# A mixture-of-experts kernel on one core: the rows of x for experts 0 to 3 come in as f32 on SyncE's queue, with the casts on ScalarE

## Chip, core and metric

The kernel runs on one core of one Trainium2 chip. The metric is the time of one execution on the device in microseconds (us); less is better. Time before: 184.42 us, the median of 5 runs that lie between 183.97 and 184.64.

## The reference

Eight experts, each with its own two weight matrices and its own 256 rows of x; two matrix products with a ReLU between them. Everything is f32 on the outside.

```python
n_experts, capacity, hidden, expert_hidden = 8, 256, 512, 2048
# x [8, 256, 512], w1 [8, 512, 2048], w2 [8, 2048, 512]
h = np.matmul(x, w1)
h = np.maximum(h, 0)
return np.matmul(h, w2).astype(np.float32)
```

An expert's w1 and w2 hold 4 MB each, its rows of x 0.5 MB and its output 0.5 MB.

## The kernel before

**Computation.** All products are made in bf16 with f32 sums in PSUM. The experts go one after the other. `first_layer(e)` (matmuls at L105) makes the hidden rows of expert e, transposed, in 64 matmuls, with ReLU on the way out of PSUM by ScalarE and VectorE in turn (L115, L113). `second_layer(e)` (L125) makes the output in 32 matmuls into two PSUM tiles, which VectorE and ScalarE copy to an f32 tile (L136, L137). The experts 5, 6 and 7 do their first layers together ahead of their second layers.

**Weights.** Each w1 and w2 is loaded by the gpsimd queue with the cast from f32 to bf16 made in the transfer (L70, L76), into pools of three buffers each (`WB = 3`). w2 of experts 6 and 7 is cut in 2 and 6 pieces. Because all of these are issued by GpSimd, they stand in one ring, in the order of the program; so do the outputs of experts 0 to 6 (`store`, L140). This ring is called the gpsimd ring below. The output of expert 7 is stored in two halves by SyncE and ScalarE.

**x.** The rows of x are handled in four groups, `GROUPS = ((0, 1), (1, 1), (2, 2), (4, 4))`: expert 0, expert 1, experts 2 and 3, experts 4 to 7. Group 0 is loaded as f32 by SyncE into `x_f` (L143) and cast to bf16 by one ScalarE copy (L154). Groups 1, 2 and 3 are loaded by the gpsimd ring with the cast in the transfer (`load_x`, L66), in rows of 4, 8 and 16 KB of f32 per partition, among the weights. `transpose_x(g)` then turns a group with TensorE (L86) through PSUM, with copies out by VectorE and ScalarE (L95, L93).

**Order.** The schedule is manual: each engine executes its instructions in the order in which the program calls them. What GpSimd is told to load first is first in the ring:

```python
    nc.sync.dma_start(x_f[:], x_rows(0))
    load_w1(0)
    make_identity(nc, identity)
    load_x(1)
    load_w2(0)
    load_w1(1)
    load_x(2)
    load_w2(1)
    load_x(3)
    load_w1(2)
    load_w2(2)
    nc.scalar.copy(x_b[0][:], x_f[:])
    transpose_x(0)
```

Later loads are issued when the buffer that they fill is free: `load_w1(3)` after `first_layer(0)`, `load_w2(3)` after `second_layer(0)`, and so on. Output tiles come from the pool `outs` of four buffers; five are used in all, for the experts (0, 1), (2, 3), (4, 5), (6) and (7).

Of the kernel before, what the change touches and what calls it, by code (L numbers as in the profile page):

```python
# [10 lines left out]
def kernel(  # L11
# [7 lines left out]
    nc = tc.nc  # L19
    P = 128  # L20
    bf = mybir.dt.bfloat16
    f32 = mybir.dt.float32
    relu = mybir.ActivationFunctionType.Relu

    E, C, H = x.shape
    F = w1.shape[2]
    MT = C // P
# [14 lines left out]
    const = ctx.enter_context(tc.tile_pool(name="const", bufs=1))  # L42
    wpool = ctx.enter_context(tc.tile_pool(name="weights", bufs=WB))
    hpool = ctx.enter_context(tc.tile_pool(name="hidden", bufs=3))
    opool = ctx.enter_context(tc.tile_pool(name="outs", bufs=4))
    ps_h = ctx.enter_context(tc.tile_pool(name="ps_h", bufs=4, space=bass.MemoryType.PSUM))
    ps_o = ctx.enter_context(tc.tile_pool(name="ps_o", bufs=4, space=bass.MemoryType.PSUM))

# [2 lines left out]

    w1_sb, w2_sb, ht, o_sb = {}, {}, {}, {}
    group_of = {e: g for g, (e0, n) in enumerate(GROUPS) for e in range(e0, e0 + n)}
    x_f = const.tile([P, MT, H], f32, name="x_f")
    x_b = [const.tile([P, n * MT, H], bf, name=f"x_b{g}") for g, (_, n) in enumerate(GROUPS)]
    xt = [const.tile([P, KT1, n, C], bf, name=f"xt{g}") for g, (_, n) in enumerate(GROUPS)]
    identity = const.tile([P, P], bf, name="identity")
# [1 line left out]
    def x_rows(g):  # L59
        e0, n = GROUPS[g]  # L60
        return x[e0:e0 + n].rearrange("e c k -> (e c) k").rearrange(
            "(p j) k -> p j k", p=P
        )

    def load_x(g):
        nc.gpsimd.dma_start(x_b[g][:], x_rows(g))  # L66

    def load_w1(e):
        w1_sb[e] = wpool.tile([P, KT1, F], bf, tag="w1", name="w1_sb")
        nc.gpsimd.dma_start(w1_sb[e][:], w1_r[e])  # L70

    def load_w2(e):
        w2_sb[e] = wpool.tile([P, KT2, H], bf, tag="w2", name="w2_sb")
        cuts = {E - 2: (0, 8, 16), E - 1: (0, 5, 9, 12, 14, 15, 16)}.get(e, (0, KT2))
        for lo, hi in zip(cuts, cuts[1:]):
            nc.gpsimd.dma_start(w2_sb[e][:, lo:hi, :], w2_r[e, :, lo:hi, :])  # L76

    def transpose_x(g, kts=range(KT1)):


        n = GROUPS[g][1]
        J = n * MT
        for kt in kts:
            pt = ps_o.tile([P, J, P], bf, tag="ps_o", name="pt_tr")
            for j in range(J):
                nc.tensor.transpose(pt[:, j, :], x_b[g][:, j, kt::KT1], identity[:])  # L86
            src = pt[:].rearrange("p (j m) (e l) -> p m e l j", m=MT, e=n)
            for mt in range(MT):
                dst = xt[g][:, kt, :, mt * P:(mt + 1) * P].rearrange(
                    "p e (l j) -> p e l j", j=J // MT  # L90
                )
                if mt % 2:
                    nc.scalar.copy(dst, src[:, mt])  # L93
                else:
                    nc.vector.tensor_copy(dst, src[:, mt])  # L95
# [44 lines left out]
        nc.gpsimd.dma_start(out_r[:, es[0]:es[-1] + 1], o_sb[es][:, :len(es)])  # L140


    nc.sync.dma_start(x_f[:], x_rows(0))  # L143
    load_w1(0)
    make_identity(nc, identity)
    load_x(1)
    load_w2(0)
    load_w1(1)
    load_x(2)
    load_w2(1)  # L150
    load_x(3)
    load_w1(2)
    load_w2(2)
    nc.scalar.copy(x_b[0][:], x_f[:])  # L154
    transpose_x(0)

    first_layer(0)
# [66 lines left out]
```

## Time and profile before

| | |
|---|---|
| median of 5 runs | 184.42 us |
| the profiled execution | 184.42 us, of which the span from the first to the last instruction is 182.6 us |
| DMA | 40.22 MB written, HBM read 71.30 MB; gpsimd ring (q0) 97.4% of 16 engines' span |
| PE (matmul) busy | 127.1 us, 70% of the span |
| VectorE, ScalarE, GpSimd busy | 32.9, 31.2 and 16.8 us |
| mean granted TensorE clock | 0.939 |

The DMA queues of a core share 16 DMA engines. In the profile q0 is the gpsimd ring, q1 SyncE's queue, q10 ScalarE's, q8 and q14 the fetches of instructions and tables. A DMA is split in packets, one per partition's row here, and each of the 16 engines carries 8 of 128 partitions; the transfer has landed when the slowest engine has finished its share. GB/s and packet sizes count what is written: a transfer that casts to bf16 reads twice what it writes.

### The profile page before, as it was taken

The page shows a single profiled execution, that of the slowest core. Times are in us where ns is not written, and L with a number is a line of the kernel's source. Part 1 is how long each engine was busy: PE and PEld are TensorE (multiplying, and loading weights), DVE is VectorE, ACT ScalarE, POOL GpSimd, SP SyncE. Part 2 cuts the span into 40 slices and gives each one's busy share as a digit, 9 for nine tenths or more (in the row PEclk, how much of TensorE's full clock was granted, in tenths as well). Part 3 has the DMA queues.
Part 4 walks back from the last instruction along what each step waited for, and adds up shares of the span by engine and source line. Part 5 has one row for each costly group of instructions (what it writes and reads, how often), then busy time and mean ns, then how long its engine had stood idle before and what let it go on. Part 6 is the DMA issues. An engine that isn't in the chain of part 4 may idle for free.

```text
span 182.6 us, 1887 instructions
## 1 busy us (share of the span) xinstructions
PE 127.1 (70%) x832; PEld 89.1 (49%) x832; DVE 32.9 (18%) x56; ACT 31.2 (17%) x58; POOL 16.8 (9%) x35
## 2 busy tenths in 40 slices
PE   0205979499492099996859493965989494997980
PEld 0104864189240079636824491424979493443430
DVE  0100340113301015402400041010334132010110
ACT  3300240113201014303300230011222131010110
POOL 7301010100102000100000006011010100110100
PEclk9999999969998559999999998798799999999998
DMA  6999999999999999999999999999999999999993
GB/s 165 212 196 223 222 223 219 190 233 219 203 228 215 219 222 215 205 219 222 223 205 219 219 189 321 229 223 208 208 223 230 208 206 313 225 210 212 214 337 138
DMA packets 5001, 40.22 MB, mean 220 GB/s; under 512 B 513, under 2 KB 769, under 8 KB 2817
## 3 DMA queue, kind: packets, MB, share of 16 engines
q0 software_dynamic: 4560, 39.06, 97.4%
q1 hardware_dynamic: 288, 0.79, 1.2%
q10 hardware_dynamic: 144, 0.26, 0.4%
q8 instruction: 6, 0.10, 0.2%
q14 instruction: 3, 0.02, 0.0%
HBM read 71.30 MB, written 4.19 MB: 413 GB/s over the span
## 4 chain that ended last, share of the span: by engine, by line
DMA 51%; PE 33%; another core or an unknown queue 9%; POOL 2%; issue 1%; ACT 0%; POOLq 0%
DMA w_sb<-in_w_dram 51%; PE pt_o L125 19%; PE pt_h L105 13%; PE pt_tr L86 1%; POOL w_sb L76 1%; POOL w_sb L70 1%; POOL x_b L66 1%; POOL out_dram L140 0%; ACT out_sb L137 0%; POOL identity masks.py:199 0%; POOL identity masks.py:197 0%; POOLq L208 0%
## 5 line engine op out<-in xcount | busy, mean ns | idle before, releaser
L105 PE MATMUL pt_h<-xt,w_sb 128*128 128x256 bf16 x512 | 65.4, 293 | 32.0 <-DMA w_sb<-in_w_dram 32.0
L105 PEld LDWEIGHTS <-w_sb 128*128 128x128 bf16 x512 | 59.6, 147 | 38.2 <-DMA w_sb<-in_w_dram 35.2
L125 PE MATMUL pt_o<-w_sb,ht_sb 128*128 128x512 bf16 x256 | 57.9, 385 | 13.2 <-DMA w_sb<-in_w_dram 13.2
L125 PEld LDWEIGHTS <-ht_sb 128*128 128x128 bf16 x256 | 25.1, 99 | 44.3 <-issue 12.9
L113 DVE TENSOR_SCALAR ht_sb<-pt_h 128x512 bf16<-128x512 f32 x32 | 22.1, 692 | 75.9 <-PE pt_h L105 75.9
L115 ACT ACTIVATE ht_sb<-pt_h 128x512 bf16<-128x512 f32 x32 | 19.1, 598 | 68.3 <-PE pt_h L105 68.3
L136 DVE COPY out_sb<-pt_o 128x512 f32<-128x512 f32 x8 | 5.5, 692 | 63.5 <-PE pt_o L125 63.5
L137 ACT COPY out_sb<-pt_o 128x512 f32<-128x512 f32 x8 | 4.7, 585 | 66.4 <-PE pt_o L125 66.4
L76 POOL DMA_DIRECT2D w_sb<-in_w_dram x14 | 7.5, 536 | 69.3 <-DMA w_sb<-in_w_dram 41.5
L70 POOL DMA_DIRECT2D w_sb<-in_w_dram x8 | 4.5, 560 | 72.4 <-PE pt_h L105 51.8
L86 PE MATMUL pt_tr<-identity,x_b 128*128 128x128 bf16 x64 | 5.4, 238 | 5.1 <-ACT x_b L154 5.1
L86 PEld LDWEIGHTS <-x_b 128*128 128x128 bf16 x64 | 4.9, 120 | 5.2 <-ACT x_b L154 5.1
L93 ACT COPY xt<-pt_tr 128x128 bf16<-128x128 bf16 (+2 forms) x16 | 5.4, 376 | 9.3 <-DVE xt L95 9.3
L95 DVE COPY xt<-pt_tr 128x128 bf16<-128x128 bf16 (+2 forms) x16 | 5.6, 384 | 5.6 <-PE pt_tr L86 5.6
L140 POOL DMA_DIRECT2D out_dram<-out_sb x4 | 2.7, 678 | 13.2 <-ACT out_sb L137 12.9
L66 POOL DMA_DIRECT2D x_b<-in_x_dram x3 | 1.7, 563 | 0.0
L154 ACT ACT_TABLE_LOAD x1 | 1.3, 1283 | 0.7 <-PEq L208 0.7
L154 ACT CAST x_b<-x_f 128x1024 bf16<-128x1024 f32 x1 | 1.0, 1044 | 2.0 <-DMA x_f<-in_x_dram 2.0
masks.py:199 POOL TENSOR_SCALAR_AFFINE_SELECT identity<-identity 128x128 bf16<-128x128 bf16 x1 | 0.3, 287 | 0.1
masks.py:197 POOL MEMSET identity<- 128x128 bf16 x1 | 0.2, 223 | 0.0
L208 POOL MEMSET const-float32-0.0<- 128x1 f32 x1 | 0.1, 93 | 0.2 <-issue 0.2
L208 POOL MEMSET const-bfloat16-1.0<- 128x1 bf16 x1 | 0.1, 95 | 0.0
(2 smaller groups left out, 0.2 us busy)
## 6 DMA issues: line engine op xcount, KB each, us to landing
w_sb<-in_w_dram POOLq DMA_DIRECT2D x14, 2048.0 KB, 47.3
out_dram<-out_sb POOLq DMA_DIRECT2D x3, 1024.0 KB, 45.6
w_sb<-in_w_dram POOLq DMA_DIRECT2D x2, 1024.0 KB, 51.4
x_b<-in_x_dram POOLq DMA_DIRECT2D x1, 1024.0 KB, 48.4
w_sb<-in_w_dram POOLq DMA_DIRECT2D x1, 640.0 KB, 47.8
x_f<-in_x_dram SPq DMA_DIRECT2D x1, 512.0 KB, 3.3
x_b<-in_x_dram POOLq DMA_DIRECT2D x1, 512.0 KB, 34.9
w_sb<-in_w_dram POOLq DMA_DIRECT2D x1, 512.0 KB, 46.5
```

The lines of the kernel that those rows point to most:

```text
L66: nc.gpsimd.dma_start(x_b[g][:], x_rows(g))
L70: nc.gpsimd.dma_start(w1_sb[e][:], w1_r[e])
L76: nc.gpsimd.dma_start(w2_sb[e][:, lo:hi, :], w2_r[e, :, lo:hi, :])
L86: nc.tensor.transpose(pt[:, j, :], x_b[g][:, j, kt::KT1], identity[:])
L93: nc.scalar.copy(dst, src[:, mt])
L95: nc.vector.tensor_copy(dst, src[:, mt])
L105: nc.tensor.matmul(ph[:, i, :], w1_sb[e][:, kt, 2 * q + i::KT2], xe[:, kt, :], start=(kt == 0), stop=(kt == KT1 - 1),)
L113: nc.vector.tensor_relu(ht[e][:, 2 * q:2 * q + 2, :], ph[:])
L115: nc.scalar.activation(ht[e][:, 2 * q:2 * q + 2, :], ph[:], relu)
L125: nc.tensor.matmul(po[mt][:], ht[e][:, kt, mt * P:(mt + 1) * P], w2_sb[e][:, kt, :], start=(kt == 0), stop=(kt == KT2 - 1),)
L136: nc.vector.tensor_copy(o[:, 0, :], po[0][:])
L137: nc.scalar.copy(o[:, 1, :], po[1][:])
```

## The change

- SyncE loads two transfers instead of one: experts 0 and 1 (1 MB, two rows of 4 KB per partition), then experts 2 and 3 (1 MB, one row of 8 KB per partition), both f32 into a tile `x_f` four times as large as before.
- ScalarE makes four casts instead of one, in a row, ahead of the transposes of group 0: expert 0, expert 1, and experts 2 and 3 in two halves. All have 1024 elements per partition.
- `load_x(1)` and `load_x(2)` leave the gpsimd ring. `load_x(3)`, for experts 4 to 7, stays.
- The pool of output tiles has three buffers instead of four.

```diff
-    opool = ctx.enter_context(tc.tile_pool(name="outs", bufs=4))
+    opool = ctx.enter_context(tc.tile_pool(name="outs", bufs=3))
...
-    x_f = const.tile([P, MT, H], f32, name="x_f")
+    x_f = const.tile([P, 4, MT, H], f32, name="x_f")
...
-    nc.sync.dma_start(x_f[:], x_rows(0))
+    nc.sync.dma_start(x_f[:, :2], x[0:2].rearrange("e (p mt) k -> p e mt k", p=P))
+    nc.sync.dma_start(x_f[:, 2:].rearrange("p e mt k -> p (e mt) k"), x_rows(2))
     load_w1(0)
     make_identity(nc, identity)
-    load_x(1)
     load_w2(0)
     load_w1(1)
-    load_x(2)
     load_w2(1)
     load_x(3)
     load_w1(2)
     load_w2(2)
-    nc.scalar.copy(x_b[0][:], x_f[:])
+    nc.scalar.copy(x_b[0][:], x_f[:, 0])
+    nc.scalar.copy(x_b[1][:], x_f[:, 1])
+    for j in (0, 1):
+        nc.scalar.copy(x_b[2][:, 2 * j:2 * j + 2, :], x_f[:, 2 + j])
     transpose_x(0)
```

## The prediction

> **What bounds the kernel now.** I read the page first (busy slices, DMA queues), then the chain of waits in order of time, then the timeline of the first microseconds, then windows over the start, then the single DMA records (packets and per-engine landings). All clock times are us from the start of the span.
>
> The page, slices and queues:
>
> ```profile
> PE   0205979499492099996859493965989494997980
> DMA  6999999999999999999999999999999999999993
> q0 software_dynamic: 4560, 39.06, 97.4%
> q1 hardware_dynamic: 288, 0.79, 1.2%
> ```
>
> The DMA engines are full in every slice but the first and the last; PE has holes all along. 97.4% of the engines' time is the gpsimd ring.
>
> The end of the chain of waits (start, us, what):
>
> ```profile
> 112.20 49.65 DMA w_sb<-in_w_dram
> 161.85 0.04 issue
> 161.90 3.61 PE pt_o L125 x16
> 165.51 1.21 another core or an unknown queue
> 166.72 0.04 issue
> 166.76 10.60 PE pt_o L125 x48
> ```
>
> Each late layer starts when its weights land, 0.04 to 0.05 us after the landing (166.72 to 166.76). The last 48 matmuls run without a gap, but from a landing; so if every landing of w1(7), w2(5) and w2(6) moves by some amount, the end moves by it. The landings are those of the slowest of 16 engines. From the landing records: w2(6)'s second half has landed on the fastest engine at 163.34, on the median at 164.52, on the slowest at 166.72. That lag of 3.4 us is built up thus: 2.15 us are there when w1(0) lands (13.73 fastest, 13.95 median, 15.71 and 15.88 the two slowest); it stays between 2.13 and 2.15 up to x of experts 4 to 7 (51.36 to 53.50); it grows by 0.96 while w1(2) lands; and by about 0.3 later, around 103 to 113.
>
> The timeline of the start, the lines that matter, with SP's DMA, the cast and the first matmuls:
>
> ```profile
> 0.74 0.37 SPq L143 DMA_DIRECT2D x_f<-in_x_dram  x1
> 1.26 0.67 POOL L70 DMA_DIRECT2D w_sb<-in_w_dram  x1 [0.81 <-POOLq L208]
> 4.03 1.04 ACT L154 CAST x_b<-x_f 128x1024 bf16<-128x1024 f32 x1 [2.01 <-DMA x_f<-in_x_dram]
> 5.82 0.91 ACT L93 COPY xt<-pt_tr 128x128 bf16<-128x128 bf16 x4 [0.75 <-DVE xt L95]
> 15.92 9.37 PE L105 MATMUL pt_h<-xt,w_sb 128*128 128x256 bf16 x64 [9.76 <-DMA w_sb<-in_w_dram]
> ```
>
> PE waits 9.76 us for w1(0), with x long ready. And windows over the start (the last two columns are the DMA share and GB/s written):
>
> ```profile
> 1.70:3.20 1.50, 0.00 (x0) 0.00 (x0) 0.00 (x0) 0.32 (x1) 1.43 (x5) 1.00 1.10 347
> 3.20:4.70 1.50, 0.00 (x0) 0.00 (x0) 0.00 (x0) 0.67 (x1) 1.50 (x4) 1.00 1.05 199
> 4.70:8.00 3.30, 1.04 (x8) 0.78 (x8) 0.86 (x4) 1.28 (x5) 1.50 (x3) 1.00 1.01 199
> 8.00:16.00 8.00, 0.08 (x1) 0.08 (x2) 0.00 (x0) 0.00 (x0) 0.00 (x0) 1.00 1.02 213
> ```
>
> From 3.2 to 8 the ring moves 199 GB/s against 213 later. The packet records say why: x_f's packets end between 3.12 and 3.63 on the engines, w1(0)'s first packets start by 3.98 on fourteen of them and at 4.67 on the last two, which so stand still for over 1.0 us; and the early w1 packets take 1.25 to 2.45 us where later ones take 1.23.
>
> **The change part by part.**
>
> *The work of the engines.* Removed from the ring: x of expert 1 and of experts 2 and 3. Their price is the step between landings of the slowest engine: 15.88 to 17.12 = 1.24 us and 36.49 to 38.95 = 2.46 us, together 3.70 us. Added on SyncE's queue: per engine 8 more rows of 4 KB and 8 rows of 8 KB. x_f's packets start 0.155 us apart, so 8 of them are 1.24 us. An 8 KB row as f32 isn't in the trace on this queue; the nearest row is a table fetch of 8 KB (0.309 to 0.322 us), which gives 8 x 0.309 = 2.47. From below, 8 x 0.307 by the step of the casting rows. Sum 3.71: net 0.0 us. The cast saves no time, since the engines are paid by what they read (4096 B in 0.155 us, 8192 in 0.307, 32768 in 1.21: 26.4 to 27 B/ns).
>
> *Where it stands in time.* x's 3.7 us come ahead of or among w1(0), w2(0) and w1(1) instead of behind w1(0) and w1(1). So w1(0), landing at 15.88, comes up to 3.7 us later, w2(0) (26.81) and w1(1) (36.49) up to 2.5 later, and from w2(1) (48.64) on all is level. PE: first layer 0 takes 9.4, second 7.1, first layer 1 about 7.5 with its transposes; the next landing that must be met is w2(1) at 48.64 and then w1(2) at 64.16, for which PE now waits 8.4 us (55.76 to 64.16). The delay is gone there at the latest. Nobody feels it before: the loads w1(3) and w2(3) that wait for these layers are issued at 25.59 and 34.23, but reach the engines only after w1(2) and w2(2), from about 73.85 on. Price nothing; if the cover were gone, at most the 3.7.
>
> *The casts.* Three more of 1.04 us each on ScalarE, 3.1 us, in the 9 us in which it idles before w1(0). But the last two wait for the second transfer, and behind them in ScalarE's queue stand its copies for the transposes of group 0, which first_layer(0) needs, and its ReLUs. How late does that transfer land? If SyncE's packets go first, at about 1.75 + 16 x 0.155 + 8 x 0.309, some 7 to 8 us: hidden. If engines take a packet of each queue in turn (as the records show for SyncE's and ScalarE's stores at 179.6 to 180.9: 0.080 us each, strictly alternating on the late engines), some 15 rows still open at 3.2 to 3.6 go one by one with 1.21 us packets of w1(0) and w2(0): 3.4 + 15 x 1.21 + 3.7 = 25. Then first_layer(0) starts at about 25 + 2.1 + 1.6 = 29, and the chain 9.4 + 0.6 + 7.1 + 7.5 + 1.1 + 7.1 ends at about 62, still ahead of 64.16. Free in both cases, the second by 2 us; past that PE has some 2.5 us of waiting in each later layer (93.26, 102.90) to catch up.
> The Trainium skill ("DMA: Bandwidth & Descriptors", section "Queues, rings and completion order") says that each engine goes round its queues packet by packet, which would make it the second case.
>
> *The idle start.* The two slowest engines stand still for 1.0 to 1.2 us between the end of x_f and the first packet of w1(0). After the change they have 16 more rows of x (3.7 us) to move in that time. Gain: 0 if the stall holds all queues of the engine; 1.2 if it is filled; at the end no more than 1.5, since the third slowest engine is 1.5 us ahead there (175.23 against 176.71 for the last piece of w2). I take 1.2: idle time with queued work to fill it.
>
> *The mixing of queues.* About 15 rows of x are written between packets of the ring. Nearest rows: a table fetch of 8 KB at 149.76 between two ring packets delays the second by 0.354 us where it should cost 0.313, so 0.04 per row; at the other end an instruction fetch of 16 KB at 54.29 took 0.975 us and the ring's packet behind it 1.40 instead of 1.23, so 0.17 to 0.19 per row. 15 x 0.04 = 0.6; 15 x 0.19 = 2.9; a gain from mixing is the idle start, counted above. I take 0.6, since the 8 KB fetch has the size of a row.
>
> *Without price:* output tiles from three buffers: the tile of expert 6 reuses that of (0, 1), stored by 115.83, that of 7 the one of (2, 3), stored by 157.06; they are written at 170.2 and 177.2. SyncE's one more issue (0.37) and GpSimd's two fewer (0.55 each) lie at the start; fewer loads are queued in front of the ring, none of them late.
>
> Sum: 0.0 - 1.2 + 0.6 = -0.6 us; the profiled execution is 184.42, equal to the median: 183.8.
> The Trainium skill ("DMA: Bandwidth & Descriptors", section "Issuing engines are not separate DMA queues") speaks against any gain: transfers of all queues run on the same engines, and another issuer saves only issue time; by that alone the sum is 0.0 and the time 184.4.
>
> **The rivals.**
> *Nothing to be filled (0.24).* Net work 0.0 and the idle start and the mixing cancel or neither is real. For: the price per byte read is equal. Time 184.1 to 184.7.
> *Mixing costs more than the idle start gives (0.33).* Every row between two ring packets takes the reading ahead away from the ring, as behind the instruction fetch: 0.06 to 0.19 each on 15 rows, 0.9 to 2.9 us, with the stall filled only in part. It decides from 0.1 us per row on. Time 184.8 to 187, the middle about 185.5. For: packets after a foreign one measured 1.38 to 1.44 in four fetches. Against: SyncE's and ScalarE's stores alternate without loss.
>
> **How the numbers follow.** Forecast 183.8 with 0.43: gains from 0.4 to 1.5 us (182.9 to 184.0). Nothing 0.24, slower 0.33. 0.2% is 0.37 us, about what a measurement of this kernel can tell from no change. The range takes in the whole gain and the mixing up to half of its upper end: 182.9 to 185.9; the forecast's own is 182.9 to 184.0.
>
> **What would show it.** Right: w1(0) lands at 18 to 20; w2(1) lands up to 1 us before 48.6, the spread between fastest and slowest engine is near 1 us instead of 2.15, w2(6) lands 0.4 to 1.5 earlier, and the last 48 matmuls follow it. Wrong: a ring packet length of 1.3 to 1.4 while x runs, w2(1) after 48.9, and all later landings late by the same amount; or the two slow engines as late as before.

## The result, and the profile after

The changed kernel takes 183.25 us (median of 45 runs, 182.82 to 183.75) against 184.37 us for the kernel before (87 runs, 182.74 to 186.19). The ratio is 0.9944, with a 95% interval from 0.9934 to 0.9954: faster by 1.1 us. The forecast was 183.8 with a range from 182.9 to 185.9. One thing stands out beside the median: nine tenths of the runs before lie between 183.28 and 185.08, after between 182.95 and 183.54. The change made the kernel quicker, and its times scatter over a third of the width.

The profiled execution took 183.26 us, with a span of 181.1. First the page after, the DMA slices and the queues:

```profile
DMA  5998998999899999999999998999999999999994
q0 software_dynamic: 4272, 38.27, 95.6%
q1 hardware_dynamic: 560, 2.36, 3.6%
HBM read 71.30 MB, written 4.19 MB: 417 GB/s over the span
```

The two loading queues take 99.2% of the engines' time together, 98.6% before; what is read from memory is the same 71.30 MB, moved at 417 GB/s over the span instead of 413. Nothing was saved in bytes. The end of the chain of waits (start, us, what):

```profile
110.41 49.99 DMA w_sb<-in_w_dram
160.41 0.04 issue
160.45 3.61 PE pt_o L125 x16
164.06 1.15 another core or an unknown queue
165.22 0.04 issue
165.26 10.61 PE pt_o L125 x48
```

From 160.41 on it has the same pieces as before with nearly the same lengths, each 1.4 to 1.5 us earlier: w2(6) has landed at 165.22 instead of 166.72, and the last 48 matmuls start at 165.26 instead of 166.76. So the gain was made before these landings, in the transfers. The span became 1.5 us shorter, the time less: the part of an execution that lies outside the span (its time less its span) is 2.12 to 2.25 us in the runs of the changed kernel, and 1.74 to 1.85 in the runs of the kernel before beside the experiments. No run shows what makes this difference of 0.37 us.

The start shows what the transfers do, first in the timeline:

```profile
0.74 0.41 SPq L143 DMA_DIRECT2D x_f<-in_x_dram  x1
1.21 0.46 SPq L144 DMA_DIRECT2D x_f<-in_x_dram  x1
5.74 1.04 ACT L153 CAST x_b<-x_f 128x1024 bf16<-128x1024 f32 x1 [3.72 <-DMA x_f<-in_x_dram]
17.61 1.99 ACT L156 CAST x_b<-x_f 128x1024 bf16<-128x1024 f32 x2 [9.87 <-DMA x_f<-in_x_dram]
19.50 0.76 ACT L93 COPY xt<-pt_tr 128x128 bf16<-128x128 bf16 x4
19.81 9.00 PE L105 MATMUL pt_h<-xt,w_sb 128*128 128x256 bf16 x64 [11.93 <-ACT xt L93]
30.02 7.07 PE L125 MATMUL pt_o<-w_sb,ht_sb 128*128 128x512 bf16 x32 [0.76 <-ACT xt L93]
38.12 6.98 PEld L105 LDWEIGHTS <-w_sb 128*128 128x128 bf16 x64 [1.53 <-DMA w_sb<-in_w_dram]
```

The first layer begins 3.9 us later than before (19.81 instead of 15.92), and not because of w1(0): ScalarE waits 9.87 us for the second transfer of x, its transposition copies stand behind those casts, and PE waits for them. It costs nothing: by first_layer(1) PE's weight loads (PEld) wait for w1(1) again (1.53 us at 38.12). And the windows over the start (last two columns: DMA share, GB/s written; f32 rows count twice what a cast counts for the same bytes read):

```profile
3.20:4.70 1.50, 0.00 (x0) 0.00 (x0) 0.00 (x0) 0.00 (x0) 1.50 (x4) 1.00 1.02 418
4.70:8.00 3.30, 1.04 (x8) 0.78 (x8) 0.72 (x4) 1.99 (x2) 0.97 (x2) 1.00 1.13 317
8.00:16.00 8.00, 0.00 (x0) 0.00 (x0) 0.15 (x1) 0.00 (x0) 0.00 (x0) 1.00 0.98 249
```

In 3.20 to 4.70 the engines write f32 rows at 418 GB/s, where before the starting ring wrote 199 and so read 398.

The packet and landing records name the difference. All 4 KB rows of x go first, and on fifteen engines two of the 8 KB rows with them; the ring's first packets start between 5.36 and 5.90 us. Not one of them is long: before, 9 ring packets took over 1.5 us at the start (four of them over 2 us), after, none. The other 8 KB rows alternate one by one with them, an 8 KB row and a 16 KB ring packet together every 1.526 us, against 1.208 for the ring packet alone. w1(0) lands on the fastest engine at 17.51, on the slowest at 17.84: a spread of 0.33 us instead of 2.15. From w2(1) on the two kernels have moved the same bytes; there the median engine is level (46.72 against 46.80 before), the mean over the engines 0.33 earlier (46.77 against 47.10), and the slowest, which sets the landing, 0.87 earlier (47.77 against 48.64). At w2(6) the mean is 0.4 earlier (164.06 against 164.45) and the slowest 1.5.

### The profile page after: what moved, and what is told of

Read it like the earlier page. It is cut to its first block, busy times and chain, and to the rows that moved or that the text cites. A ratio compares the mean times of both kernels' runs of the same rounds, so it can differ in the third digit from the quotient of the medians.

```text
span 181.1 us, 1891 instructions
## 1 busy us (share of the span) xinstructions
PE 130.2 (72%) x832; PEld 90.4 (50%) x832; DVE 32.9 (18%) x56; ACT 34.0 (19%) x61; POOL 15.7 (9%) x33
## 3 DMA queue, kind: packets, MB, share of 16 engines
HBM read 71.30 MB, written 4.19 MB: 417 GB/s over the span
## 4 chain that ended last, share of the span: by engine, by line
DMA 47%; PE 39%; another core or an unknown queue 7%; POOL 2%; issue 1%; ACT 1%; DVE 1%; POOLq 0%
DMA w_sb<-in_w_dram 47%; PE pt_o L125 20%; PE pt_h L105 17%; PE pt_tr L86 1%; ACT xt L93 1%; POOL w_sb L76 1%; DVE ht_sb L113 0%; POOL out_dram L140 0%; ACT out_sb L137 0%; POOL w_sb L70 0%; DVE xt L95 0%; POOL identity masks.py:199 0%; POOL identity masks.py:197 0%; POOLq L210 0%
## 5 line engine op out<-in xcount | busy, mean ns | idle before, releaser
L105 PE MATMUL pt_h<-xt,w_sb 128*128 128x256 bf16 x512 | 66.3, 296 | 28.0 <-DMA w_sb<-in_w_dram 16.1
L105 PEld LDWEIGHTS <-w_sb 128*128 128x128 bf16 x512 | 60.3, 148 | 34.7 <-DMA w_sb<-in_w_dram 29.1
L125 PE MATMUL pt_o<-w_sb,ht_sb 128*128 128x512 bf16 x256 | 60.0, 395 | 10.8 <-DMA w_sb<-in_w_dram 8.4
L125 PEld LDWEIGHTS <-ht_sb 128*128 128x128 bf16 x256 | 25.7, 101 | 43.4 <-issue 15.1
L156 ACT CAST x_b<-x_f 128x1024 bf16<-128x1024 f32 x2 | 2.0, 1042 | 9.9 <-DMA x_f<-in_x_dram 9.9
L153 ACT CAST x_b<-x_f 128x1024 bf16<-128x1024 f32 x1 | 1.0, 1045 | 3.7 <-DMA x_f<-in_x_dram 3.7
L154 ACT CAST x_b<-x_f 128x1024 bf16<-128x1024 f32 x1 | 1.0, 1042 | 0.0
L66 POOL DMA_DIRECT2D x_b<-in_x_dram x1 | 0.6, 558 | 0.0
```

The costliest lines, as they stand in the source:

```text
L105: nc.tensor.matmul(ph[:, i, :], w1_sb[e][:, kt, 2 * q + i::KT2], xe[:, kt, :], start=(kt == 0), stop=(kt == KT1 - 1),)
L125: nc.tensor.matmul(po[mt][:], ht[e][:, kt, mt * P:(mt + 1) * P], w2_sb[e][:, kt, :], start=(kt == 0), stop=(kt == KT2 - 1),)
```

## The experiments

**The theories.** The *spread* of a load is the time between its landings on the fastest and the slowest engine; a *long* packet is a ring packet of over 1.5 us near the start. *Cover*: the gpsimd ring has a bad start, a few microseconds in which some engines begin late and packets take too long; rows of x on SyncE's queue give the engines work until that is over, and any rows would do. *Alternation*: the 8 KB rows between ring packets keep the engines even. *GpSimd*: the ring starts badly because GpSimd is issuing the next loads (2.46 to 6.2 us) meanwhile. *Leaving the ring*: what helps is that x is no longer in it.

**Each half alone.**

```diff
 e1_x01, against the kernel before:
-    x_f = const.tile([P, MT, H], f32, name="x_f")
+    x_f = const.tile([P, 2, MT, H], f32, name="x_f")
...
-    nc.sync.dma_start(x_f[:], x_rows(0))
+    nc.sync.dma_start(x_f[:, :2], x[0:2].rearrange("e (p mt) k -> p e mt k", p=P))
...
-    load_x(1)
...
-    nc.scalar.copy(x_b[0][:], x_f[:])
+    nc.scalar.copy(x_b[0][:], x_f[:, 0])
+    nc.scalar.copy(x_b[1][:], x_f[:, 1])
 e2_x23, against the kernel before:
-    opool = ctx.enter_context(tc.tile_pool(name="outs", bufs=4))
+    opool = ctx.enter_context(tc.tile_pool(name="outs", bufs=3))
...
-    x_f = const.tile([P, MT, H], f32, name="x_f")
+    x_f = const.tile([P, 3, MT, H], f32, name="x_f")
...
-    nc.sync.dma_start(x_f[:], x_rows(0))
+    nc.sync.dma_start(x_f[:, 0], x_rows(0))
+    nc.sync.dma_start(x_f[:, 1:].rearrange("p e mt k -> p (e mt) k"), x_rows(2))
...
-    load_x(2)
...
-    nc.scalar.copy(x_b[0][:], x_f[:])
+    nc.scalar.copy(x_b[0][:], x_f[:, 0])
+    for j in (0, 1):
+        nc.scalar.copy(x_b[2][:, 2 * j:2 * j + 2, :], x_f[:, 1 + j])
```

> Only half of the change: x of experts 0 and 1 as f32 on SyncE in one transfer (16 rows of 4 KB per engine), x of experts 2 and 3 cast on the gpsimd ring as before. Cover theory (the ring's start-up stall on single engines passes unseen while rows of SyncE's queue are on the engines): the gain is all here; w1(0) lands on all engines within 0.5 us (2.15 before), time 183.2 to 183.5. Theory of the alternation (the 8 KB rows written one by one between the ring's packets keep the engines even): these rows are gone, so the stall is back, spread of w1(0) 1.5 to 2.2 us, time 184.2 to 184.6. GpSimd theory (the stall comes from GpSimd writing the next loads' descriptors at 2.5 to 6.2 us while the ring starts): cured as far as the ring's first packet starts after 5 us; as it does, 183.2 to 183.5.

> The other half: x of expert 0 as before, x of experts 2 and 3 as f32 on SyncE in 8 KB rows, x of expert 1 cast on the gpsimd ring as before; output pool of 3 as in the changed kernel. Cover theory and alternation theory: cured, 183.2 to 183.5, spread of w1(0) under 0.5 us. GpSimd theory: the ring's first packets start at 3.4 to 4.6 us, in the middle of GpSimd's issues, so part of the stall stays: spread 1 to 2 us, time 183.8 to 184.5.

Measured: e1_x01 183.36 us, ratio 0.9961 (0.9943 to 0.9978); e2_x23 183.43 us, ratio 0.9958 (0.9939 to 0.9977); the kernel before on that chip 184.18. Each half does what the whole does within their intervals. The spread of w1(0) is 0.39 and 0.47 us, and neither has a long packet. The timelines show how differently they get there (e1_x01, then e2_x23: casts and first matmuls):

```profile
5.68 1.04 ACT L153 CAST x_b<-x_f 128x1024 bf16<-128x1024 f32 x1 [3.66 <-DMA x_f<-in_x_dram]
15.34 8.84 PE L105 MATMUL pt_h<-xt,w_sb 128*128 128x256 bf16 x57 [7.51 <-DMA w_sb<-in_w_dram]
```

```profile
10.46 1.99 ACT L156 CAST x_b<-x_f 128x1024 bf16<-128x1024 f32 x2 [5.26 <-DMA x_f<-in_x_dram]
16.48 7.69 PE L105 MATMUL pt_h<-xt,w_sb 128*128 128x256 bf16 x55 [10.19 <-DMA w_sb<-in_w_dram]
```

e1_x01 has no 8 KB rows and nothing that alternates, its x is through on each engine before the ring's first packet there (4.90 to 5.32 us), and its first layer starts even earlier than before (15.34): the alternation theory falls. In e2_x23 the ring's first packets start at 5.34 us with rows of x ahead of them. e1_x01 keeps four output buffers and e2_x23 has three, so the pool makes no visible difference.

**GpSimd's issues out of the way.**

```diff
 e4_gpwait, against the kernel before:
+    idle = const.tile([P, 2048], f32, name="idle")
...
     load_w1(0)
     make_identity(nc, identity)
+    for _ in range(3):
+        nc.gpsimd.memset(idle[:], 0.0)
     load_x(1)
```

> The kernel before, with GpSimd busy for some 5 to 6 us (three memsets of a scratch tile) between the identity and load_x(1): after load_w1(0) nothing more is issued on the ring until 8 us or so. GpSimd theory: w1(0)'s packets take 1.23 us from the first on, spread under 0.5 us, time 183.2 to 183.5. Cover theory: nothing covers the ring's start, spread 1.5 to 2.5 us as before, time 184.2 to 184.6; a plain loss would be possible only if the ring ran dry, which it does not before 13.7 us.

Measured: 184.84 us, ratio 1.0026 (1.0000 to 1.0053). In the kernel before, GpSimd issues six more loads from 2.46 us on, one after the other; the first and the last of them:

```profile
2.46 0.55 POOL L66 DMA_DIRECT2D x_b<-in_x_dram  x1
5.61 0.59 POOL L70 DMA_DIRECT2D w_sb<-in_w_dram  x1
```

The timeline of e4_gpwait shows the pause:

```profile
1.25 0.67 POOL L71 DMA_DIRECT2D w_sb<-in_w_dram  x1 [0.81 <-POOLq L211]
2.46 5.53 POOL L148 MEMSET idle<- 128x2048 f32 x3
8.49 0.54 POOL L77 DMA_DIRECT2D w_sb<-in_w_dram  x1
```

GpSimd issues no DMA from 1.9 to 7.9 us, and still two engines are late: w1(0) lands at 13.80 on the median engine, and on the last two at 15.27 and 16.59, the slowest 2.8 us behind the median (1.9, 2.5 and 0.4 in three profiles of the kernel before); the two longest early ring packets took 2.2 and 2.6 us. So the stall doesn't need GpSimd's issues. But there are only 3 long packets here, against 9 to 17 in the three profiles of the kernel before, so a part of the lengthening on the others may go with the issues; one profile doesn't show it.

**Rows that nobody needs.**

```diff
 e3_dummy, against the kernel before:
+    x_d = const.tile([P, MT, H], f32, name="x_d")
...
     nc.sync.dma_start(x_f[:], x_rows(0))
+    nc.sync.dma_start(x_d[:], x_rows(1))
```

> The kernel before with nothing moved, and 8 more rows of 4 KB per engine on SyncE's queue behind x_f: x of expert 1 is loaded a second time, into a tile that nobody reads; 1.24 us more work for every engine. Cover theory: the rows hide the ring's start, w1(0) lands on all engines within 0.5 us, and the time is 184.3 + 1.24 - 1.1 = 184.4 (184.1 to 184.7). Rival, that the gain comes from x leaving the ring (fewer or larger transfers in it): no gain, only the work, 185.5 (185.2 to 185.8), spread 1.5 to 2.5 us.

Measured: 184.37 us, ratio 1.0009 (0.9986 to 1.0032) to the kernel before (184.07). The windows of e3_dummy over the start:

```profile
3.20:4.70 1.50, 0.00 (x0) 0.00 (x0) 0.00 (x0) 0.77 (x1) 1.50 (x4) 1.00 1.66 505
4.70:8.00 3.30, 1.04 (x8) 0.78 (x8) 0.86 (x4) 1.18 (x5) 1.50 (x3) 1.00 0.81 169
8.00:16.00 8.00, 0.88 (x5) 0.71 (x6) 0.00 (x0) 0.00 (x0) 0.53 (x1) 1.00 1.09 227
```

Half a megabyte more to read, 1.24 us of every engine, and no measurable loss: it pays for itself. (A packet's whole time counts in the window where it starts, hence 1.66 and 0.81.) The rows last to 4.84 us, the ring's first packets follow at 4.47 to 4.84, no packet is long, and w1(0) lands with a spread of 0.48. Nothing has left the ring in this kernel, so that theory falls. With e1_x01 and e2_x23 this shows the gain to come with rows on SyncE's queue ahead of the ring's first packets; which rows they are doesn't matter.

**Is it the ring's first use, or the first microseconds of a run?**

```diff
 e7_latering, against the changed kernel:
+    idle = const.tile([P, 2048], f32, name="idle")
...
+    for _ in range(2):
+        nc.gpsimd.memset(idle[:], 0.0)
     load_w1(0)
 e9_prime_late, against e7_latering:
+    prime = const.tile([P, 128], bf, name="prime")
...
+    nc.gpsimd.dma_start(prime[:], x_rows(0)[:, 0, :128])
     for _ in range(2):
         nc.gpsimd.memset(idle[:], 0.0)
```

> The changed kernel with two memsets of a scratch tile (3.7 us) on GpSimd ahead of load_w1(0): the ring is issued to at 5 us instead of 1.26, when most of x's rows are through. Cold ring theory (two engines get or fetch the ring's first descriptors some 3 us after the issue instead of 1.5, whenever that is): x's rows end at about 6.8, the two engines stand still again until 8 or later; w1(0) spread 1 to 2.5 us, and all engines idle up to 0.7 us: time 184.5 to 185.5. Cold memory theory (whatever reads in the first 5 us of a run is slow on some engines): no stall at two engines, spread under 0.5 us, only the common idle time: 183.6 to 184.1.

> As e7_latering (the changed kernel, GpSimd paused for 3.7 us ahead of load_w1(0)), but the ring is used once before the pause: a transfer of 512 B of x per partition (256 B written) into a tile that nobody reads. If the stall belongs to the ring's first use, it passes with the small transfer while x's rows are on the engines: w1(0) lands on all engines within 0.5 us (1.56 in e7_latering, two engines 1.4 behind the median), time 183.0 to 183.3. If it comes with every start of the ring on engines that the other queue has left, two engines are late by 1.4 again, time as e7_latering, 183.4.

Measured: e7_latering 183.40 us, ratio 0.9945 (0.9922 to 0.9967); e9_prime_late 183.20 us, ratio 0.9947 (0.9928 to 0.9966). The pause and the ring's first use (e7_latering, then e9_prime_late):

```profile
0.74 3.67 POOL L147 MEMSET idle<- 128x2048 f32 x2 [0.29 <-POOLq L213]
4.35 0.67 POOL L71 DMA_DIRECT2D w_sb<-in_w_dram  x1
```

```profile
1.26 0.67 POOL L147 DMA_DIRECT2D prime<-in_x_dram  x1 [0.81 <-POOLq L215]
1.92 3.68 POOL L149 MEMSET idle<- 128x2048 f32 x2
5.55 0.53 POOL L72 DMA_DIRECT2D w_sb<-in_w_dram  x1
```

The load was issued at 4.35, not at the 5 us expected. In e7_latering the last row of x ended at 7.6, fourteen engines started the ring by then, and the last two landed w1(0) at 19.11 where the median is 17.71. In e9_prime_late, with the ring used once beforehand, w1(0) is issued later still, and lands on all engines between 17.65 and 18.18. Both ran once more with a profile:

> A second look at e7_latering (changed kernel, ring first used at 4.35 us). If the ring's first use makes the stall: again one or more engines over 0.8 us behind the median at the landing of w1(0). If the two late engines of the first look were chance: all within 0.5 us.

> A second look at e9_prime_late (the same pause, ring used once before it). If the stall belongs to the first use: no engine over 0.5 us behind the median at the landing of w1(0). If not: as e7b_latering.

Again two engines late in e7b_latering (19.25 and 19.30, median 17.82) and none in e9b_prime_late (17.63 to 18.15); long packets: 2 and 4 with the late first use, 0 and 0 with the primed ring. So in these four profiles the stall goes with the first use of the ring, and not with the first microseconds of a run.

The times, though, missed the expectation: 183.40 instead of 184.5 to 185.5, and the second profiled executions took 182.85 (stalled) and 183.86 (not). So a stall of 1.4 us on two engines is not worth 1.4 us of time. The landing records show one reason. Each run has six instruction fetches, packets of 16 KB of which each holds one engine for 0.88 to 0.98 us. In the changed kernel the one at 34.25 us leaves one engine behind: w1(1) lands there at 38.08, on the next at 37.22. In e7_latering a fetch at 34.28 takes its 0.9 us from an engine that was not late. So the slowest engine, 1.27 us later than in the changed kernel at w1(0), is only 0.42 later at w2(1) (48.19 against 47.77): the stall cost only what it exceeded that later delay by. At w2(6) the slowest was 1.5 behind the median in both (165.72 against 164.21, and 165.22 against 163.70). And a small loss is hidden: the span of e7_latering is 0.7 us shorter than that of the kernel before on its chip, that of e9_prime_late 1.05; but 1.80 us of e7_latering's time lie outside the span, 1.95 of e9_prime_late's.

**Priming without cover.**

```diff
 e10_prime, against the kernel before:
+    prime = const.tile([P, 128], bf, name="prime")
...
+    nc.gpsimd.dma_start(prime[:], x_rows(0)[:, 0, :128])
     load_w1(0)
```

> The kernel before with only that small transfer put ahead of load_w1(0); x as before, so x_f's rows end at 3.1 to 3.7 us and cover nothing after that. If the first use costs some 3 us on single engines whatever is queued, the small transfer starts the clock at the same 1.26 us and w1(0) is issued 0.6 later: stall as before, spread of w1(0) 1.5 to 2.5 us, time 184.0 to 184.6. If the stall is one of large first packets, the small ones take it: spread under 0.6 us, 183.2 to 183.6.

Measured: 184.36 us, ratio 1.0017 (0.9996 to 1.0039): no gain. On two engines the small packets are late too (4.25 to 4.79 us, where the others end by 3.9), w1(0) has 12 long packets, and its spread is 1.30. Here priming helped only where other work ran while it took effect, as in e9_prime_late.

**The form of the first transfer.**

```diff
 e5_split, against the changed kernel:
-    nc.sync.dma_start(x_f[:, :2], x[0:2].rearrange("e (p mt) k -> p e mt k", p=P))
+    nc.sync.dma_start(x_f[:, 0], x_rows(0))
+    nc.sync.dma_start(x_f[:, 1], x_rows(1))
```

> The changed kernel with x of experts 0 and 1 in two transfers of one 4 KB row per partition each, instead of one transfer of two rows per partition. In the changed kernel the first packet on each engine took 0.64 to 1.05 us, in the kernel before 0.17 to 0.56. If the two-row form makes that, all landings move by -0.5 to -0.6 us: 182.7. If it is the start of the memory or chance: 183.2 to 183.3.

Measured: 183.57 us, ratio 0.9967 (0.9950 to 0.9985), not better than the changed kernel's 0.9944. The first packets were shorter (0.16 to 0.66 us), and nothing came of it at the end. The two-row form is no loss.

**The kernel before, twice more.**

> The kernel before once more, for a second look at the start. If the stall of one or two engines at the ring's start makes its time, then its time and the lag of the slowest engine at w1(0) go together: 183 with a lag under 1 us against the median engine, 184.4 with 2, 185.4 with 3. If the lag has nothing to do with it, no such order.

> As b1_before: a third look at the start of the kernel before.

Measured: 184.17 and 184.29 us; the slowest engine's lag to the median at w1(0) was 2.5 and 0.4 us. The order that was expected isn't there, so these runs don't show that the slowest engine's lag at w1(0) makes the time. In b2_before the median itself is 1.9 us late (15.84 instead of 13.95): the stall hit more than half of the engines, in b1_before three, in the first profile two. What the three profiles do agree in is the landing of w2(6) on the slowest engine, 166.72, 166.46 and 166.60, each 17.7 us ahead of the time, and 9 to 17 long packets, where the changed kernel and the four others that had x's rows or rows in their place ahead of the ring (e1_x01, e2_x23, e3_dummy, e5_split) have none.

Over all fourteen profiles the slowest engine, a little later, does tell the two kinds of kernel apart. Without rows ahead of the ring (the kernel before three times, e4_gpwait, e10_prime) w2(1) lands at 48.64 to 49.85 and w2(6) at 166.46 to 167.00; with them, and no added load, at 47.58 to 48.34 and 165.15 to 166.01 (e3_dummy, with its 1.24 us of added loads, at 48.78 and 166.89). The scatter goes the same way: the standard deviation of the times is 0.42 to 0.7 us without such rows and 0.18 to 0.36 with them.

No version that was run beats the changed kernel: those with the start covered and no added loads lie at 183.2 to 183.6.

## Why the prediction was right

*What bounds the kernel, and the end moving with the landings of w2(6)*: right; 1.50 us earlier landing, 1.50 us earlier last matmuls, 1.5 us shorter span. But the prediction took the time to follow the span one to one; 0.37 us more outside the span were no term of its sum.

*Work of the engines, net 0.0*: right. The 8 KB rows cost 1.526 - 1.208 = 0.318 us each, the table fetch had said 0.309; the median engine is level at w2(1) within 0.08 us.

*Idle start, -1.2*: that rows of x fill the ring's bad start was right, by e1_x01, e2_x23 and e3_dummy. Its size was near: the slowest engine's landing gained 0.87 at w2(1) and 1.50 at w2(6). But it was described too narrowly. It is not only two engines standing still: ring packets on many engines were lengthened as well, and the number of engines hit differs from run to run (two, three and nine of 16 in three profiles). That two late engines alone make the price isn't shown: e7_latering has two and keeps most of the gain, e10_prime is 0.5 behind the median at w1(0) and has none. The scatter of the kernel before probably comes from this start; the prediction did not see it in its five times.

*Mixing, +0.6*: the term that was mis-sized. Taken as 15 rows at 0.04; measured 8 KB rows at 0.318 against 0.309, on at most 8 rows of an engine: under 0.1 us. Its row was misread, too: in the kernel before, the ring packet behind the table fetch at 149.76 starts at 150.08, a delay of 0.319 and not 0.354, so that row gave 0.01 and not 0.04. With 0.1 the sum is -1.1 and the time 183.3, as measured, but this agreement is partly luck: the span fell by 1.5, and 0.37 was lost outside it. The count failed because all 16 rows of 4 KB were written ahead of the ring's first packet, which started at 5.36 and not at 3.2; the ring waited behind them instead of taking turns. Later the turns were strict, as the row of the stores had said. The Trainium skill's turn by packets ("DMA: Bandwidth & Descriptors", section "Queues, rings and completion order") agrees with the 8 KB rows from 5.4 us on, one ring packet to one row; whether the ring had work ready before that, no run shows.

*Late x and first layer, no price*: right as to the price. The second transfer landed at 17.58, between the 7 to 8 (whose own terms add up to 6.7) and the 25 that were given, for the same reason; first_layer(0) started at 19.81 instead of 29, and by w1(1) PE waited for weights again.

*What would show it*: w1(0) landed at 17.84, a little ahead of the 18 to 20 named; the spread fell to 0.33, further than the 1 us named; w2(1) came 0.87 earlier and w2(6) 1.50.

The rival "mixing costs more" fell with the 0.318 and with ring packets of 1.226 us beside x. The rule that another issuer saves only issue time (same page, section "Issuing engines are not separate DMA queues") holds for the median engine, which gained nothing by w2(1); the mean and the slowest engine gained 0.33 and 0.87 there, from the start of the transfers and not from issue time.

**Open.** Why one or more engines see the ring's first packets late, which engines these are, and why the ring's first packet waits until 5.3 us when x's rows are queued and comes at 3.2 when they end: no run here shows it. Nor what adds 0.37 us outside the span. How much of the gain is the slowest engine and how much the mean isn't separated either: in the one pair of profiles 0.4 of the 1.5 us at w2(6) is the mean, and e4_gpwait has lost on the slowest alone (mean at w2(6) 164.08, slowest 167.00, time of that run 185.36).

## What to carry to other kernels

When a kernel is bound by transfers, look at how far apart the 16 engines land, not only at how full they are: the slowest engine sets each landing, and a lag from the first microseconds can be carried to the end, as far as later delays on other engines don't exceed it. Give the engines plain loads on another queue until the gpsimd ring has started (here until about 4.8 us), even if these loads only replace casting ones of the same bytes. And take a wide scatter of the times as a hint that something at random is on the critical path. Before a small gain is put down to a cause, look at the part of the time outside the span: here it moved by a third of the gain.

## What the runs showed of the hardware that was not expected

- The first use of the gpsimd ring left one or more of 16 engines 1.4 to 2.8 us behind the median (e4_gpwait, e7_latering, b1_before), also when it came at 4.35 us instead of 1.26. One small transfer before, with other work to cover it, removed this (two of two profiles).
- 0.5 MB of additional loads at the start, 1.24 us of every engine, cost no measurable time (e3_dummy, ratio 1.0009).
- Two queues alternated packet by packet almost without loss: 1.526 us for an 8 KB f32 row and a 16 KB casting packet together, against 1.208 for the packet and 0.309 for the row alone.
- Each of the six instruction fetches of a run (16 KB, 0.88 to 0.98 us) holds one engine and can make it the slowest. So a stall of 1.4 us on two engines at the start (e7_latering) was only 0.42 us at w2(1).
